# Attention layer of a two-block network: GpSimd's arithmetic moved to TensorE and VectorE, the gate and second modulation as products with a repeated column

## The chip, the cores and the metric

The program runs on one core of one Trainium2 chip. The metric is the device time of one execution in microseconds (us), lower is better. The engines go by the profile's names: PE is TensorE, PEld its weight loads, DVE VectorE, ACT ScalarE, POOL GpSimd, SP SyncE, which only issues transfers.

## The reference

The network has two blocks; the change lies in the first one, in the part ahead of its experts. With `D = 1024`, 512 tokens, and float32 throughout:

```python
mod = silu(c) @ w_ada + b_ada
shift1, scale1, gate1, shift2, scale2, gate2 = split(mod, 6)
h = rms_norm(x, norm1_g) * (1 + scale1) + shift1
proj = h @ w_in                              # six parts of 512 columns
o_a = dilated_mixture_attention(...)         # 8 heads of 64
o_b = differential_attention(...)            # 4 heads of 2 x 64
x = x + gate1 * (concat(o_a, o_b) @ w_out)
h2 = rms_norm(x, norm2_g) * (1 + scale2) + shift2
x = x + gate2 * moe_ffn(h2)                  # 32 experts, 4 for each token
```

`c` is one vector, so the last four parts of `mod` (gate1, shift2, scale2, gate2) are four vectors of 1024, each the product of a vector of 1024 with a 1024 x 1024 piece of `w_ada`. The kernel needs each of them repeated on all 128 partitions.

## The kernel before

The program has four phases; the change touches only `phase1`, the attention layer and the routing that follows it. What comes after (the experts, the second block's branches and its product-key layer) is the same code.

Float32 precision is kept in the large products by splitting each operand into a rounded part and a rest: ScalarE writes the rounded half (`wh`, `hTh`), another engine subtracts it from the original (`wl`, `hTl`), and TensorE makes three products (`mm3`, L167). Smaller products use plain float32.

**First part of phase 1 (about the first 72 us, written out in order).** The normalised input is transposed; for each of eight blocks of 128 columns `mod_block` (L383) computes the shift and scale. The shift goes through a VectorE product and sum, the scale through eight TensorE products with a two-column `sc2`, or for the five blocks in `PMOD` through GpSimd products and sums whose column sum TensorE takes in `mod_apply` (L418). Meanwhile the first 512 columns of `w_in` are multiplied.

**Second part (a planner).** `race` (L99) runs some thirty generators. Each yields a time on a modelled clock, in which every instruction is given a fixed cost per engine and per column; the generator with the lowest time goes next, and the order in which they emit instructions becomes the order of each engine's queue. Its lanes are: `ws.lane` (loads, rounds and splits `w_in`), `chunks` (ten half chunks of `w_in`, 96 products each), `norms`, the attention pairs (`pair_b` for the differential half, `pair_a` for the dilated one: `prep`, `scores`, `weigh`), `projects` and `third` (the product with `w_out`, times the gate, added to `x`), `roots`, `second` (the second normalisation with shift and scale) and routing.

**PSUM.** It has eight banks, which a counter deals out: `take(ps=...)` waits until enough are free. A half chunk takes two, a pair's scores two, its weighting three (a differential pair keeps two of them until its output has been turned), an output product one or two.

**The vectors of the second modulation.** `mods2` (L778) loads for each part eight weight tiles of 128 x 1024 (SP's queue, L786); GpSimd multiplies each with its column of `silu(c)` (L790; ScalarE at the even tiles of part 3, L788) and adds it to a running sum (L793). `mod_rows` (L799) then sums each part over the partitions by a product with ones (L809), and VectorE adds the bias row (L814). `projects` waits until three of the four parts are ready (L868); part 3 (gate2) begins when `x` is loaded again (L781).

**GpSimd's other work in this phase.** `WStream` (L196) takes an engine for each split: 22 of the 24 tiles of `w_in` (L341) and 5 of the 8 tiles of `w_out` (L836) are subtracted on GpSimd. So are most of the residual sums (L858, L915) and half of the sums of the second normalisation (L941).

The pages (30 tiles of 128 x 1024) are handed round by name: a load waits on SP's queue until the tile that it overwrites has been read.

Of the kernel before, what the change touches and what calls it, by code (L numbers as in the profile page):

```python
# [18 lines left out]
P = 128  # L19
# [286 lines left out]
def phase1(K):  # L306
# [31 lines left out]
    srcs = [wsrc(kp * 2, 2, first * 512, 512) for kp in range(4)]  # L338
    for c, half in HALVES:
        srcs += [wsrc(kq * 4, 4, c * 512 + half * 256, 256) for kq in range(2)]  # L340
    ws = WStream(K, srcs, 3, 2, eng=lambda i: nc.gpsimd if i < 4 or i >= 4 + len(EXTRA) and i % LOP == 0 else None)  # L341


    wada = []
# [38 lines left out]
    def mod_block(k):  # L383

        bm = K.bank("bm")
        w = wada[k][0]
        v.tensor_tensor(out=w, in0=w, in1=sc[:, :, None].to_broadcast([P, KC, P]), op=ALU.mult)
        acc = K.small([P, P], tag="mac", bufs=5)
        v.tensor_reduce(out=acc, in_=w.rearrange("p a c -> p c a"), axis=AX.X, op=ALU.add)
        w = wada[k][1]  # L390
        wada[k] = acc1 = None
        if k in PMOD:
            tt = nc.gpsimd.tensor_tensor
            tt(out=w, in0=w, in1=sc[:, :, None].to_broadcast([P, KC, P]), op=ALU.mult)
            tt(out=w[:, 0:4, :], in0=w[:, 0:4, :], in1=w[:, 4:8, :], op=ALU.add)
            tt(out=w[:, 0:2, :], in0=w[:, 0:2, :], in1=w[:, 2:4, :], op=ALU.add)
            acc1 = K.small([P, P], tag="mac", bufs=5)
            tt(out=acc1, in0=w[:, 0, :], in1=w[:, 1, :], op=ALU.add)
        else:
            for i in range(KC):  # L400
                nc.tensor.matmul(bm[:, 2:4], w[:, i, :], sc2[:, i, :], start=i == 0, stop=i == KC - 1)
        return (acc, acc1), bm

    m = [mod_block(0)]
    xT = [K.page(shape=[P, 2, T], name="xT") for _ in range(4)]
# [10 lines left out]
        return hT[k // 2][0][:, k % 2, :], hT[k // 2][1][:, k % 2, :]  # L416

    def mod_apply(k, acc, bm):  # L418
        for i, a in enumerate(acc):
            if a is not None:  # L420
                nc.tensor.matmul(bm[:, 2 * i:2 * i + 2], a, K.onesF[:, 0:2], start=True, stop=True)
        m = K.small([P, 2], tag="mcol", bufs=4)
        v.tensor_tensor(out=m, in0=bm[:, 0:4].rearrange("p (j t) -> p j t", t=2)[:, :, 0],
                        in1=bcol.rearrange("p (a k) -> p a k", a=2)[:, :, k], op=ALU.add)
        a1 = K.small([P, 1], tag="a1", bufs=4)
        v.scalar_tensor_tensor(a1, m[:, 1:2], 1.0, g1c[:, k:k + 1], op0=ALU.add, op1=ALU.mult)
        src = xT[k // 2][:, k % 2, :]
        hi, lo = hTk(k)
        act.activation(src, src, AF.Identity, bias=m[:, 0:1], scale=a1)
        act.copy(hi, src)  # L430
# [63 lines left out]
    def take(**n):  # L494

        while any(free[i] < n[i] for i in n):
            yield
        give(**{i: -n[i] for i in n})

    def give(**n):  # L500
        for i in n:
            free[i] += n[i]
# [274 lines left out]

    def mods2():  # L778

        for part in range(4):  # L780
            while part == 3 and len(xs) < NB:  # L781
                yield
            g = K.hold(name="gate2") if part == 3 else K.page(name="gm")
            for k in range(KC):
                w = K.page(name="wada")
                nc.sync.dma_start(out=w, in_=I["w_ada"][k * P:(k + 1) * P, (part + 2) * D:(part + 3) * D])  # L786
                if (part, k % 2) in MACT:
                    act.activation(w if k else g, w, AF.Copy, scale=sc[:, k:k + 1])  # L788
                else:
                    nc.gpsimd.tensor_tensor(out=w if k else g, in0=w, in1=sc[:, k:k + 1].to_broadcast([P, D]), op=ALU.mult)  # L790
                yield
                if k:
                    nc.gpsimd.tensor_tensor(out=g, in0=g, in1=w, op=ALU.add)  # L793
                yield
            gm.append(g)
            g = w = None
        yield

    def mod_rows(parts):  # L799
        while len(gm) < parts[-1] + 1:  # L800
            yield
        for part in parts:
            br = K.page(name="brow")
            act.dma_start(out=br, in_=row_bcast(I["b_ada_row"][:, part * D:(part + 1) * D], D))
            bs = []
            yield from take(ps=2)
            for half in range(2):
                bs.append(K.bank("gm"))
                nc.tensor.matmul(bs[half], K.onesF, gm[part][:, half * 512:half * 512 + 512], start=True, stop=True)  # L809
            yield  # L810
            yield
            for half in range(2):
                s = slice(half * 512, (half + 1) * 512)
                v.tensor_tensor(out=gm[part][:, s], in0=bs[half], in1=br[:, s], op=ALU.add)  # L814
            bs = br = None
            give(ps=2)
            yield
            if part == 2:
                g2r = K.page(name="g2r")
                act.dma_start(out=g2r, in_=row_bcast(I["norm2_g"], D))  # L820
                v.scalar_tensor_tensor(gm[2], gm[2], 1.0, g2r, op0=ALU.add, op1=ALU.mult)
                g2r = None
            rows.append(part)
            yield

    def lane(*gs):
        for g in gs:
            yield from g
# [4 lines left out]
            return [(dst.rearrange("p (k n) -> p k n", n=512), I["w_out"][k0 * P:(k0 + 2) * P, half * 512:half * 512 + 512].rearrange("(k p) n -> p k n", p=P))]  # L833
        return f

    wos = WStream(K, [osrc(k0 + j, half) for k0, js in ((4, (0, 2)), (0, (0,)), (2, (0,))) for half in range(2) for j in js], 2, 0, eng=lambda i: nc.gpsimd if i % WOE else None)  # L836
    xs = []

    def project(tb, half, wo, k0):
        hs = slice(half * 512, (half + 1) * 512)  # L840
        s = slice(tb * P, (tb + 1) * P)
        yield from take(ps=1)
        b = K.bank("wo")
        n = 2 * len(wo)
        for j in range(n):
            k = k0 + j
            ws = slice(j % 2 * 512, j % 2 * 512 + 512)
            K.mm3(b, (oT[k // 2][0][:, k % 2, s], oT[k // 2][1][:, k % 2, s]), (wo[j // 2][0][:, ws], wo[j // 2][1][:, ws]), j == 0, j == n - 1)
            if j == n - 1:
                yield  # L850
            elif j % 2:
                yield K.clock.free["tensor"] - PEA
        t = K.small([P, 512], tag="sq", bufs=2)
        v.tensor_tensor(out=t, in0=b, in1=gm[0][:, hs], op=ALU.mult)
        b = None
        give(ps=1)
        yield
        (v if k0 == 2 and half in ADDV else nc.gpsimd).tensor_tensor(out=xs[tb][:, hs], in0=xs[tb][:, hs], in1=t, op=ALU.add)  # L858
        t = None

    def projects():
# [26 lines left out]
    def third(tb):  # L888
# [18 lines left out]
        for half in range(2):  # L907
            yield ends[half]
            hs = slice(half * 512, (half + 1) * 512)
            t = K.small([P, 512], tag="sq", bufs=2)  # L910
            v.tensor_tensor(out=t, in0=bs[half], in1=gm[0][:, hs], op=ALU.mult)
            bs[half] = None
            give(ps=1)
            yield
            (v if half in ADDV else nc.gpsimd).tensor_tensor(out=xs[tb][:, hs], in0=xs[tb][:, hs], in1=t, op=ALU.add)  # L915
            yield
            act.activation(t, xs[tb][:, hs], AF.Square, accum_out=sums[i][0][:, tb % 2, half:half + 1])
            t = None
# [13 lines left out]
    def second(tb):  # L932
# [4 lines left out]
        for half in range(2):  # L937
            hs = slice(half * 512, (half + 1) * 512)
            v.scalar_tensor_tensor(h2[:, hs], xs[tb][:, hs], rss[tb // 2][:, tb % 2:tb % 2 + 1], gm[2][:, hs], op0=ALU.mult, op1=ALU.mult)
            yield  # L940
            (nc.gpsimd if half in H2P else v).tensor_tensor(out=h2[:, hs], in0=h2[:, hs], in1=gm[1][:, hs], op=ALU.add)  # L941
            yield None if half else K.clock.free["vector"]
        nc.sync.dma_start(out=K.h2d[tb * P:(tb + 1) * P, :], in_=h2)
        yield from take(ps=2)
# [54 lines left out]
    br = K.const([P, NE], name="br")  # L999
    nc.scalar.dma_start(out=br, in_=row_bcast(I["b_router"], NE))  # L1000
    B, A = [pair_b(h) for h in range(4)], [pair_a(p) for p in range(4)]
    race(K.clock, third(0), third(1), third(2), third(3), prefetch(), roots(0), roots(1), *[second(tb) for tb in range(NB)], ws.lane(WSA), split_out(), norms(), *(lane(B[0],A[0]),lane(B[1],A[1]),lane(B[2],A[2]),lane(B[3],A[3])), lane(chunks(), projects()), lane(mod_rows((0, 1, 2)), mod_rows((3,))), mods2())

    K.gate2 = gm[3]


CAP = 128
MACT = [(p, k) for p in range(3, 4) for k in range(1)]
ADDV, WOE = (1,), 3
HTV = ()  # L1010
RACT = True
PF, MLA = (8, 4, 4), (10, 6, 6, 1, 4)
# [4 lines left out]
UPACE, BV = 5.1, 3  # L1017
VB, VB2 = 4.0, 1.0
START = "a0 r01 n0 t0 a1 l0 r12 n1 t1 a2 l1 r23 n2 t2 a3 l2 w0 r34 n3 t3 l3"
LOP, ANRM, BNRM = 1, (0, 1), True  # L1020
HALVES = [(c, half) for c in (4, 5) for half in range(2)] + [(c, half) for half in range(2) for c in (0, 1, 2)]
SD, ES, QK, PEA, LAT = 1, 6, 2, 0.5, 0.2
H2P = (0,)
SMALL = 0.07
EXTRA = (5, 7)
WLA, WSA, WOA = 2, 1, 2
PMOD, ML, MA = (1, 2, 4, 5, 7), 3, 2
OFF = 10000.0
BIG = 4096.0

# [1614 lines left out]
```

## Time and profile before

| what | value |
|---|---|
| median of 3 runs | 3761.43 us (3748.43 to 3765.33) |
| the profiled execution | 3763.79 us, span 3762.0 us |
| PE busy | 3390.4 us (90%) |
| DVE busy | 3237.6 us (86%) |
| ACT busy | 1845.3 us (49%) |
| POOL busy | 1096.1 us (29%) |
| mean granted clock of TensorE | 0.947 |

A span is the time from the first to the last instruction. Busy time is the union of an engine's instructions; matmuls overlap, so a busy PE need not be at its peak. The clock is a share of 2.4 GHz. A row of instructions by group reads: line, engine, operation, what is written from what, shape, count | busy us, mean ns of one | idle time of the engine just before them and what ended it. A plain float32 product stands as two records in PE's rows.

### The profile page before, as it was taken

The numbers are of one execution on the slowest core, as the hardware profiler recorded it, in microseconds if no ns is written. First come the engines' busy times: TensorE is split into PE (matmuls) and PEld (weight loads), VectorE is DVE, ScalarE is ACT, GpSimd is POOL, SyncE is SP. The second block draws the span as 40 slices with busy tenths as digits, with TensorE's granted clock in tenths as the row PEclk, the third lists the DMA queues.
The fourth block names the chain that finished last, engine by engine and source line by source line (L and its number), as shares of the span: only waits on it lengthen the run. The fifth ranks groups of instructions, "written<-read, shape, count | busy, mean of one in ns | idle before, by whom it ended". The sixth has DMA issues, their size and how long they took to land. (4 is left out here: it accounts for less than half of the span.)

```text
span 3762.0 us, 51865 instructions
## 1 busy us (share of the span) xinstructions
PE 3390.4 (90%) x17053; PEld 2884.7 (77%) x17053; DVE 3237.6 (86%) x5729; ACT 1845.3 (49%) x2684; POOL 1096.1 (29%) x742
## 2 busy tenths in 40 slices
PE   6788789898999999999488899899889889999999
PEld 6776667667777888887377777798889889888887
DVE  7888789999898999998688776499999986799988
ACT  3233367666665677776234453333344445333333
POOL 5545501101110111111334440023223230456554
PEclk8878889999999999999699899899999999999999
DMA  6224369888997899997511112366779787999997
GB/s 216 85 85 157 129 232 327 295 306 304 334 317 252 319 356 368 351 366 282 182 51 51 51 52 100 104 208 216 237 241 309 251 291 248 334 340 342 345 340 260
DMA packets 453989, 906.05 MB, mean 241 GB/s; under 512 B 37810, under 2 KB 188978, under 8 KB 453586
## 3 DMA queue, kind: packets, MB, share of 16 engines
q1 hardware_dynamic: 333488, 692.66, 53.0%
q0 software_dynamic: 46368, 151.03, 11.1%
q10 hardware_dynamic: 73858, 59.00, 4.7%
q8 instruction: 136, 2.23, 0.2%
q14 instruction: 139, 1.14, 0.1%
HBM read 845.42 MB, written 74.96 MB: 245 GB/s over the span
## 5 line engine op out<-in xcount | busy, mean ns | idle before, releaser
L84 DVE TENSOR_TENSOR wl<-wr,wh 128x1024 fp32r<-128x1024 f32 x1106 | 1346.4, 1252 | 150.9 <-ACT wh L84 145.1
L84 ACT CAST wh<-wr 128x1024 fp32r<-128x1024 f32 x1133 | 1132.8, 1049 | 166.7 <-DVE wl L84 44.0
L84 PE MATMUL ft<-HT,wh 128*128 128x384 f32 (+1 forms) x2304 | 620.7, 350 | 4.9 <-ACT wh L84 4.9
L84 PE MATMUL out<-wh,HT 128*128 128x512 f32 x1536 | 473.3, 389 | 1.5 <-ACT HT L84 1.5
L84 PE MATMUL gu<-wl,exh 128*128 128x512 f32 x1056 | 417.6, 395 | 22.5 <-DVE wl L84 22.3
L84 PEld LDWEIGHTS ft<-HT,wh 128*128 128x128 f32 x2304 | 424.4, 193 | 14.8 <-ACT wh L84 5.5
L84 PE MATMUL ft<-HT,wl 128*128 128x384 f32 (+1 forms) x1152 | 402.8, 350 | 26.0 <-DVE wl L84 25.8
L84 PE MATMUL gu<-wh,exh 128*128 128x512 f32 x1056 | 420.6, 398 | 0.3 <-ACT wh L84 0.3
L84 PE MATMUL gu<-wh,exl 128*128 128x512 f32 x1056 | 413.7, 392 | 0.0
L84 PEld LDWEIGHTS out<-wh,HT 128*128 128x128 f32 x1536 | 288.2, 188 | 61.9 <-ACT HT L84 1.8
L2454 POOL DMA_INDIRECT ug<-in_peer_u,et x128 | 167.6, 1309 | 453.5 <-DVE sv L84 241.5
L84 PE MATMUL out<-wl,HT 128*128 128x512 f32 x768 | 298.8, 389 | 0.0
L2454 POOL DMA_INDIRECT ug<-in_peer_v,et x128 | 156.3, 1221 | 362.0 <-DVE x L84 240.0
L84 PEld LDWEIGHTS gu<-wl,exh 128*128 128x128 f32 x1056 | 199.5, 189 | 74.8 <-DVE wl L84 35.6
L84 PEld LDWEIGHTS ft<-HT,wl 128*128 128x128 f32 x1152 | 221.8, 193 | 40.7 <-DVE wl L84 35.6
L1317 POOL DMA_INDIRECT ybuf<-y,dst x33 | 93.3, 2827 | 505.1 <-DVE y L84 505.1
L84 PE MATMUL qkv<-wl,hTh 128*128 128x256 f32 (+1 forms) x736 | 227.2, 309 | 14.4 <-DVE wl L84 11.8
L1244 POOL DMA_INDIRECT xg<-h2d,tok x33 | 42.9, 1300 | 675.8 <-PE dn L84 478.1
L84 PE MATMUL qkv<-wh,hTh 128*128 128x256 f32 (+1 forms) x736 | 235.1, 319 | 2.0 <-ACT wh L84 2.0
L84 PEld LDWEIGHTS gu<-wh,exh 128*128 128x128 f32 x1056 | 199.8, 189 | 45.7 <-ACT wh L84 3.0
L84 PE MATMUL dn<-wl,ath 128*128 128x512 f32 x528 | 213.5, 404 | 22.9 <-DVE wl L84 20.2
L84 PEld LDWEIGHTS gu<-wh,exl 128*128 128x128 f32 x1056 | 199.3, 189 | 41.8
(481 smaller groups left out, 6952.8 us busy)
## 6 DMA issues: line engine op xcount, KB each, us to landing
wr<-in_w_gate_up SPq DMA_DIRECT2D x512, 512.0 KB, 6.5
wr<-in_w_down SPq DMA_DIRECT2D x256, 512.0 KB, 6.4
wr<-in_u_t SPq DMA_DIRECT2D x128, 512.0 KB, 4.3
wr<-in_peer_v SPq DMA_DIRECT2D x128, 512.0 KB, 6.1
wr<-in_w_in SPq DMA_DIRECT2D x68, 512.0 KB, 3.5
wada<-in_w_ada SPq DMA_DIRECT2D x48, 512.0 KB, 4.3
Sd<-us ACTq DMA_DIRECT2D x128, 192.0 KB, 4.7
Gd<-gst ACTq DMA_DIRECT2D x12, 2048.0 KB, 15.7
```

The lines of the kernel that those rows point to most:

```text
L84: return f(*a, **kw)
L1244: nc.gpsimd.indirect_dma_start(out=self.xg, out_offset=None, in_=K.h2d[:, :], in_offset=bass.IndirectOffsetOnAxis(ap=self.tok[:, :1], axis=0),
L1317: st = nc.gpsimd.indirect_dma_start(out=self.rows, out_offset=bass.IndirectOffsetOnAxis(ap=self.dst[:, :1], axis=0), in_=y, in_offset=None ...
L2454: nc.gpsimd.indirect_dma_start(out=r, out_offset=None, in_=tab, in_offset=bass.IndirectOffsetOnAxis(ap=et[:, m:m + 1], axis=0), bounds_che ...
```

## The change

GpSimd no longer does any arithmetic in phase 1. The five mod blocks of `PMOD` use the TensorE products of the others. All splits, residual sums and modulation sums go to VectorE. `mods2` is rewritten: a tile `scb` holds `silu(c)` with each column repeated 128 times, and for each part eight weight tiles are multiplied by it on TensorE in plain float32, 512 columns at a time, accumulating in two PSUM banks that are taken before the first and given back after the last; the result stands on all partitions at once. Two tiles are loaded ahead (`MLD`), and a tile's products are at least 6 us of the planner's clock after the previous ones (`MPACE`). The bias row and the gain row are loaded at the start of a part. `mod_rows` is gone.

```diff
-    ws = WStream(K, srcs, 3, 2, eng=lambda i: nc.gpsimd if i < 4 or i >= 4 + len(EXTRA) and i % LOP == 0 else None)
+    ws = WStream(K, srcs, 3, 2)
...
-        wada[k] = acc1 = None
-        if k in PMOD:
-            tt = nc.gpsimd.tensor_tensor
-            tt(out=w, in0=w, in1=sc[:, :, None].to_broadcast([P, KC, P]), op=ALU.mult)
-            tt(out=w[:, 0:4, :], in0=w[:, 0:4, :], in1=w[:, 4:8, :], op=ALU.add)
-            tt(out=w[:, 0:2, :], in0=w[:, 0:2, :], in1=w[:, 2:4, :], op=ALU.add)
-            acc1 = K.small([P, P], tag="mac", bufs=5)
-            tt(out=acc1, in0=w[:, 0, :], in1=w[:, 1, :], op=ALU.add)
-        else:
-            for i in range(KC):
-                nc.tensor.matmul(bm[:, 2:4], w[:, i, :], sc2[:, i, :], start=i == 0, stop=i == KC - 1)
-        return (acc, acc1), bm
+        wada[k] = None
+        for i in range(KC):
+            nc.tensor.matmul(bm[:, 2:4], w[:, i, :], sc2[:, i, :], start=i == 0, stop=i == KC - 1)
+        return acc, bm
...
     def mods2():
...
+        scb = K.page(shape=[P, KC, P], name="scb")
+        v.tensor_copy(scb, sc[:, :, None].to_broadcast([P, KC, P]))
+        t = 0.0
+        pages = []
+
+        def fetch(i):
+            part, k = divmod(i, KC)
+            w = K.page(name="wada")
+            nc.sync.dma_start(out=w, in_=I["w_ada"][k * P:(k + 1) * P, (part + 2) * D:(part + 3) * D])
+            pages.append(w)
+
         for part in range(4):
             while part == 3 and len(xs) < NB:
                 yield
...
             br = K.page(name="brow")
             act.dma_start(out=br, in_=row_bcast(I["b_ada_row"][:, part * D:(part + 1) * D], D))
...
+            for i in range(MLD):
+                fetch(part * KC + i)
+            t = max(t + MPACE, K.clock.end + MPACE)
+            yield t
+            yield from take(ps=2)
+            bs = [K.bank("gm") for _ in range(2)]
+            for k in range(KC):
+                if k + MLD < KC:
+                    fetch(part * KC + k + MLD)
+                w = pages.pop(0)
+                for half in range(2):
+                    nc.tensor.matmul(bs[half], scb[:, k, :], w[:, half * 512:half * 512 + 512], start=k == 0, stop=k == KC - 1)
+                w = None
+                t = max(t + MPACE, K.clock.end)
+                yield t if k < KC - 1 else None
+            g = K.hold(name="gate2") if part == 3 else K.page(name="gm")
+            for half in range(2):
+                s = slice(half * 512, (half + 1) * 512)
+                v.tensor_tensor(out=g[:, s], in0=bs[half], in1=br[:, s], op=ALU.add)
...
-    wos = WStream(K, [...], 2, 0, eng=lambda i: nc.gpsimd if i % WOE else None)
+    wos = WStream(K, [...], 2, 0)
...
-        (v if k0 == 2 and half in ADDV else nc.gpsimd).tensor_tensor(out=xs[tb][:, hs], in0=xs[tb][:, hs], in1=t, op=ALU.add)
+        v.tensor_tensor(out=xs[tb][:, hs], in0=xs[tb][:, hs], in1=t, op=ALU.add)
...
-            (v if half in ADDV else nc.gpsimd).tensor_tensor(out=xs[tb][:, hs], in0=xs[tb][:, hs], in1=t, op=ALU.add)
+            v.tensor_tensor(out=xs[tb][:, hs], in0=xs[tb][:, hs], in1=t, op=ALU.add)
...
-            (nc.gpsimd if half in H2P else v).tensor_tensor(out=h2[:, hs], in0=h2[:, hs], in1=gm[1][:, hs], op=ALU.add)
+            v.tensor_tensor(out=h2[:, hs], in0=h2[:, hs], in1=gm[1][:, hs], op=ALU.add)
...
-    race(K.clock, ..., lane(mod_rows((0, 1, 2)), mod_rows((3,))), mods2())
+    race(K.clock, ..., mods2())
...
+MLD, MPACE = 2, 6.0
```

## Rows read from the trace of the kernel before

**Rows 1.** By stretch, us: length, busy PE, PEld, DVE, ACT, POOL; clock; DMA; GB/s

```profile
0.00:72.00 72.00, 41.80 (x180) 35.82 (x180) 52.85 (x71) 25.44 (x35) 43.86 (x32) 0.86 0.63 233
72.00:108.00 36.00, 35.96 (x267) 34.65 (x268) 29.03 (x40) 12.24 (x20) 19.78 (x10) 0.95 0.42 130
72.00:345.00 273.00, 222.94 (x1439) 201.47 (x1440) 227.81 (x441) 88.69 (x205) 137.98 (x63) 0.82 0.31 102
345.00:470.00 125.00, 98.33 (x468) 77.94 (x466) 93.96 (x221) 46.09 (x118) 74.76 (x52) 0.83 0.42 149
```

**Rows 2.** Instructions by group, VectorE, 0 to 470 us

```profile
L84 DVE TENSOR_SCALAR e<-e,rd 128x128 f32<-128x128 f32 (+3 forms) x48 | 44.2, 978 | 0.1
L84 DVE TENSOR_TENSOR raw<-raw,qrs 128x256 f32<-128x256 f32 x32 | 31.7, 1040 | 0.1
...
L84 DVE TENSOR_TENSOR wada<-wada,silc 128x1024 f32<-128x1024 f32 x8 | 16.3, 2041 | 0.0
...
L84 DVE TENSOR_TENSOR rqa<-qrs 128x16 f32<-128x16 f32 x24 | 12.5, 520 | 0.5
...
L84 DVE TENSOR_TENSOR rsqa<-obr 128x4 f32<-128x4 f32 x12 | 10.1, 838 | 0.2
L84 DVE SCALAR_TENSOR_TENSOR rsqa<-rsqa,rsqv 128x4 f32<-128x4 f32 x15 | 9.6, 639 | 0.3
...
L84 DVE TENSOR_TENSOR h<-h,gm 128x512 f32<-128x512 f32 x4 | 2.7, 680 | 0.0
```

**Rows 3.** Timeline of VectorE: start us, us, instruction; places up to 312 us

```profile
32.56 1.21 DVE L84 TENSOR_TENSOR wada<-wada,silc 128x1024 f32<-128x1024 f32 x1
...
102.16 0.17 DVE L84 TENSOR_TENSOR rqa<-qrs 128x16 f32<-128x16 f32 x1
...
106.25 7.40 DVE L84 TENSOR_TENSOR raw<-raw,qrs 128x256 f32<-128x256 f32 x4
...
117.88 1.43 DVE L84 TENSOR_TENSOR raw<-raw,qrs 128x256 f32<-128x256 f32 x4
...
303.16 7.08 DVE L84 TENSOR_SCALAR e<-e,rd 128x128 f32<-128x128 f32 x4
...
310.85 1.26 DVE L84 TENSOR_SCALAR e<-e,rd 128x128 f32<-128x128 f32 x4
```

**Rows 4.** Timeline of GpSimd, 110 to 122 us

```profile
110.52 2.52 POOL L84 TENSOR_TENSOR gm<-gm,wada 128x1024 f32<-128x1024 f32 x1
119.18 2.37 POOL L84 TENSOR_TENSOR wl<-wr,wh 128x1024 fp32r<-128x1024 f32 x1 [6.15 <-ACT wh L84]
```

**Rows 5.** Waits of TensorE, 0 to 470 us: total us, times, longest

```profile
PE ot L84 <- DVE op L84: 15.2, 2, 14.6
...
PE h2t L84 <- POOL h L84: 9.1, 1, 9.1
```

**Rows 6.** Instructions by group, GpSimd, 0 to 470 us

```profile
L84 POOL TENSOR_TENSOR wl<-wr,wh 128x1024 fp32r<-128x1024 f32 x27 | 67.3, 2494 | 107.5 <-ACT wh L84 79.3 <-DVE rsqa L84 19.8 <-issue 8.4
```

**Rows 7.** The page, costliest groups: the same subtraction on VectorE, whole span

```profile
L84 DVE TENSOR_TENSOR wl<-wr,wh 128x1024 fp32r<-128x1024 f32 x1106 | 1346.4, 1252 | 150.9 <-ACT wh L84 145.1
```

**Rows 8.** Timeline of TensorE, 345 to 359 us

```profile
345.19 1.88 PE L84 MATMUL gm<-gm,onesF 128*128 128x512 f32 x4
...
354.86 3.78 PE L84 MATMUL gm<-gm,onesF 128*128 128x512 f32 x4
```

**Rows 9.** Instructions by group, TensorE, 0 to 470 us

```profile
L84 PE MATMUL bm<-silc,wada 128*128 128x2 f32 x48 | 8.9, 317 | 16.7 <-DMA wada<-in_w_ada 16.7
```

**Rows 10.** The page, DMA issues: count, KB each, median us to landing

```profile
wada<-in_w_ada SPq DMA_DIRECT2D x48, 512.0 KB, 4.3
```

**Rows 11.** The page, 40 slices of the span: TensorE's busy tenths

```profile
PE   6788789898999999999488899899889889999999
```

**Rows 12.** Instructions by group, TensorE, 180 to 200 us

```profile
L84 PE MATMUL ob<-vh,pt 128*128 128x128 f32 x20 | 3.8, 279 | 0.0
L84 PE MATMUL s<-qkh,qkh 64*128 64x256 f32 (+3 forms) x7 | 3.1, 444 | 0.0
```

More of the change, by code (lines that the diff above doesn't have):

```diff
@@ L418, in mod_apply @@
     def mod_apply(k, acc, bm):
-        for i, a in enumerate(acc):
-            if a is not None:
-                nc.tensor.matmul(bm[:, 2 * i:2 * i + 2], a, K.onesF[:, 0:2], start=True, stop=True)
+        nc.tensor.matmul(bm[:, 0:2], acc, K.onesF[:, 0:2], start=True, stop=True)
         m = K.small([P, 2], tag="mcol", bufs=4)
@@ L782, in mods2 @@
                 yield
[L783 to L802, printed above, removed]
             br = K.page(name="brow")
             act.dma_start(out=br, in_=row_bcast(I["b_ada_row"][:, part * D:(part + 1) * D], D))
[L805 to L817, printed above, removed]
             if part == 2:
@@ L820, in mod_rows @@
                 act.dma_start(out=g2r, in_=row_bcast(I["norm2_g"], D))
-                v.scalar_tensor_tensor(gm[2], gm[2], 1.0, g2r, op0=ALU.add, op1=ALU.mult)
+            for i in range(MLD):
[17 more added lines that the diff above has]
+                v.tensor_tensor(out=g[:, s], in0=bs[half], in1=br[:, s], op=ALU.add)
+            bs = br = None
+            give(ps=2)
+            if part == 2:
+                v.scalar_tensor_tensor(g, g, 1.0, g2r, op0=ALU.add, op1=ALU.mult)
                 g2r = None
+            gm.append(g)
             rows.append(part)
+            g = None
             yield
@@ L834, in osrc @@
         return f
-    wos = WStream(K, [osrc(k0 + j, half) for k0, js in ((4, (0, 2)), (0, (0,)), (2, (0,))) for half in range(2) for j in js], 2, 0, eng=lambda i: nc.gpsimd if i % WOE else None)
+    wos = WStream(K, [osrc(k0 + j, half) for k0, js in ((4, (0, 2)), (0, (0,)), (2, (0,))) for half in range(2) for j in js], 2, 0)
     xs = []
@@ L1001, in phase1 @@
     B, A = [pair_b(h) for h in range(4)], [pair_a(p) for p in range(4)]
-    race(K.clock, third(0), third(1), third(2), third(3), prefetch(), roots(0), roots(1), *[second(tb) for tb in range(NB)], ws.lane(WSA), split_out(), norms(), *(lane(B[0],A[0]),lane(B[1],A[1]),lane(B[2],A[2]),lane(B[3],A[3])), lane(chunks(), projects()), lane(mod_rows((0, 1, 2)), mod_rows((3,))), mods2())
+    race(K.clock, third(0), third(1), third(2), third(3), prefetch(), roots(0), roots(1), *[second(tb) for tb in range(NB)], ws.lane(WSA), split_out(), norms(), *(lane(B[0],A[0]),lane(B[1],A[1]),lane(B[2],A[2]),lane(B[3],A[3])), lane(chunks(), projects()), mods2())
     K.gate2 = gm[3]
 CAP = 128
-MACT = [(p, k) for p in range(3, 4) for k in range(1)]
-ADDV, WOE = (1,), 3
+MLD, MPACE = 2, 6.0
 HTV = ()
@@ L1019 @@
 START = "a0 r01 n0 t0 a1 l0 r12 n1 t1 a2 l1 r23 n2 t2 a3 l2 w0 r34 n3 t3 l3"
-LOP, ANRM, BNRM = 1, (0, 1), True
+ANRM, BNRM = (0, 1), True
 HALVES = [(c, half) for c in (4, 5) for half in range(2)] + [(c, half) for half in range(2) for c in (0, 1, 2)]
 SD, ES, QK, PEA, LAT = 1, 6, 2, 0.5, 0.2
-H2P = (0,)
 SMALL = 0.07
@@ L1026 @@
 WLA, WSA, WOA = 2, 1, 2
-PMOD, ML, MA = (1, 2, 4, 5, 7), 3, 2
+ML, MA = 3, 2
 OFF = 10000.0
```

## The prediction

> **What bounds the kernel now.** I read the page first: TensorE and VectorE are both busy for most of the span, GpSimd for little of it. The diff touches only the first attention layer, which ends when the router starts, some 470 us into the span. So the second view is busy time by stretch, cut at 72 us (the end of the first product), 345 us (the last head of the differential half has been turned) and 470 us [rows 1]. In the long stretch from 72 to 345 us VectorE is busy 228 of 273 us and TensorE 223, at a mean clock of 0.82. GpSimd is busy 138 us, and the layer has no other heavy user of it. In no stretch is any engine full except TensorE from 72 to 108 us: 35.96 of 36 us, clock 0.95. That is what TensorE does when nothing holds it up.
>
> The third view, VectorE by groups [rows 2], shows what is odd. Instructions on 4 or 16 columns last 0.5 to 0.8 us on average, and 256 columns last 1.04 us. The timeline tells why [rows 3, 4]. Four products `raw<-raw,qrs` from 106.25 us on take 7.40 us while GpSimd runs its two-input instructions; the same four from 117.88 us on, with GpSimd idle for 6.15 us until 119.18, take 1.43 us. Four `e<-e,rd` take 7.08 us at 303 us, and 1.26 us at 311 us. So much of VectorE's busy time is waiting for GpSimd. TensorE waits behind it in turn: 15.2 us of its idle time is for `op`, computed by just such a VectorE chain, and 9.1 us for a sum on GpSimd itself [rows 5].
>
> **What the waiting is worth.** Count times (mean minus undisturbed duration), with the undisturbed one from rows 3:
> - `e<-e,rd`: 48 x (0.978 - 0.32) = 31.6 us (1.26 us for four widths gives 0.32)
> - `raw`: 32 x (1.040 - 0.36) = 21.8
> - `rqa<-qrs`: 24 x (0.520 - 0.17) = 8.4
> - the two `rsqa` groups: 12 x (0.838 - 0.17) + 15 x (0.639 - 0.17) = 8.0 + 7.0
> - `wada<-wada,silc`: 8 x (2.041 - 1.21) = 6.6
>
> Together 83 us of VectorE time up to 470 us. Smaller groups of the same kind are left out, so this is a lower bound.
>
> **What is added to VectorE.** 27 subtractions `wl` leave GpSimd [rows 6], at 1.25 us each on VectorE [rows 7]: 33.8 us. 20 residual sums and 4 sums of the second modulation at 0.68 us, the `h<-h,gm` row [rows 2]: 16.3 us. One broadcast copy of 1024 columns is not in the trace: between 0.6 us (half of 1.21) and 1.25 us (two inputs of that width); I take 1.2, the nearer form. Together 51 us, so VectorE gets at least 32 us lighter.
>
> **What is added to TensorE.** Each of four vectors of 1024 is now summed by 8 x 2 float32 products of 512 columns: 64 products. The same form stands in the trace as `gm<-gm,onesF`, two records to a product: four records take 1.88 us at the full clock, thus 0.94 us a product, and 3.78 us at the half clock, 1.89 us a product [rows 8]. Parts 0 to 2 put 48 x 0.94 = 45 us into the middle stretch. Part 3 puts 16 x 0.94 = 15 us after 345 us, from where the 8 column-sum products (7.5 us) go away. The five mod blocks of the first stretch take 8 products, two records each, 80 in all; 48 such records were busy 8.9 us [rows 9], so 15 us.
>
> The Trainium skill (Perfetto Trace Analysis, Engine Utilization) says that float32 in two passes halves TensorE's output rate. By it a product of 512 columns would take an estimated 2 x 512 / 2.4 GHz = 0.43 us and the 48 would cost 20 us. The trace disagrees: 0.94 us stands in a row of the same form, so this reading gets no chance of its own.
>
> **What moves on the queues.** The 32 loads `wada` stay on SP's queue, two ahead now, at least 6 us of the planner's time apart; one lands in 4.3 us [rows 10], so a TensorE product waiting for one should find it there. If it doesn't, everything behind it on TensorE waits too, where earlier only GpSimd waited; 0 to 4.3 us per late load, and I take 0 because of the lead. The bias row's loads on ACT's queue are issued before the products rather than after, which can only help. One to two more 4 KB pages of 30 are held (the broadcast, a second weight tile); if a page were missing, SP's queue would hold the loads of `w_in` behind it. I take 0 for the same lead. Of GpSimd's 257 us up to 470 us [rows 1] none is left on a path but its wait for `h`, counted below.
>
> **The sum by stretches.** 0 to 72 us: VectorE loses 6.6 us and gets 4 x 1.25 = 5.0; TensorE has 30 us idle for the 15 us. I take -2.
>
> 72 to 345 us: VectorE falls from 228 to about 180, so TensorE becomes the tighter one. Its 223 us at clock 0.82 are 223 x 0.82 / 0.95 = 192 us at the clock of the undisturbed stretch; with 45 us added, 237 us. It had 50 us idle. With none left the stretch takes 237 us (-36), with half 262 (-11), with all 287 (+14). I take 15 us of idle time, because the waits that I see in it end at VectorE chains stretched several times over, and because the new products don't depend on those chains: 252 us, -21.
>
> 345 to 470 us: the wait of 9.1 us for GpSimd's `h` mostly goes; VectorE gets 5 + 20 + 4 instructions (23 us) against about a fifth of its 83 us; TensorE's net 7.5 us have 27 us of idle time around them. I take -5.
>
> Together -28 us. The expert stage that follows has TensorE at 8 to 9 tenths throughout [rows 11], so an earlier start is passed on, and I take it in full. The profiled execution took 3763.8 us with a span of 3762.0; 3763.8 - 28 = 3735.8. The median of the runs is 2.4 us below the profiled one: 3733 us.
>
> **The rivals.**
> *TensorE gives it all back.* Its idle time is a matter of dependencies, not of slow VectorE work: 25 to 45 us of it stay, and the middle stretch ends between -11 and +9. For it: 45 us of products are added to an engine already busy four fifths of the time. Against it: the idle waits end at VectorE and GpSimd. Time: 3745 to 3765.
>
> *TensorE packs fully.* No idle time is left in the middle stretch, and the last one loses 8: -46, 3715 us. For it: 72 to 108 us ran so. Against: many short chains meet later.
>
> *PSUM banks run short, slower.* The new products hold two of eight banks for eight weight tiles, some 48 us for each part by the 6 us pace, where the old ones held two for one short product. From 180 to 200 us scores `s` and weighting `ob` run side by side [rows 12]; by the code these hold 2 and 3 banks, and a half chunk in work 2 more. With two more there are nine, so a score or a weighting must wait for the other while a part lasts. Each overlap lost costs up to the 20 us of that stretch. Two lost cancel the gain (3745); three, one for each part, give 3733 + 60 = 3793. For it: the count of banks. Against: chunk products and the new ones fill TensorE meanwhile, and the bound on the path is only felt if the head chain sets the end.
>
> The Trainium skill (Perfetto Trace Analysis, Optimization Strategy) names repeated bubbles on the engine that should be full as a sign of too little PSUM or SBUF. No run here shows it yet; it is what I would look for.
>
> *The waiting isn't GpSimd's.* If VectorE's long instructions came from something else, 51 us would be added to it, a part on the path: +30 us, 3791. The paired rows speak against it.
>
> **Chances.** 0.5% is 19 us, about what a measurement of this kernel can tell from no change. Forecast 0.50, full packing 0.12, TensorE gives it back 0.23, banks 0.12, not GpSimd 0.03. Faster by over 0.5% (under 3742): 0.62; same: 0.23; slower (over 3780): 0.15. Range 3692 to 3785: below it VectorE would need more than the bound of 83 us off the path, above it three overlaps lost.
>
> **What would show it.** Right: no GpSimd arithmetic before 470 us; `rqa` and `rsqa` at 0.17 us and `raw` near 0.4 in the means; the last turned head at about 320 us rather than 345; TensorE's idle time in the middle under 25 us and its clock above 0.85. Wrong: TensorE idle as much as before beside undisturbed VectorE instructions (banks or dependencies), or `s` and `ob` no longer in the same stretch (banks), or TensorE waiting for `wada`.

## The result, and the profile after

The changed kernel takes 3704.1 us (median of 4 runs, 3700.4 to 3711.7) where the kernel before took 3763.4 us beside it (4 runs, 3748.4 to 3774.5): a ratio of 0.9849, 95% interval 0.9829 to 0.9869, 59 us faster. Timed again (run `e12_after_again` below) it was 0.9849 again. The forecast was 3733 us, with 3715 as one of its rivals.

The profiled execution took 3711.7 us, with a span of 3709.6 us. The 40 slices of its page:

```profile
PE   7999699898999999995688999999888889999999
...
PEclk9999799999999999997799999999999999999999
```

The second to fourth slice (93 to 371 us) are now at 9 tenths, where the kernel before has 7, 8 and 8 [rows 11].

The last turned differential head, at which the forecast cut the layer, comes in another order now (its `ot` at 226 us, 118 us earlier, where the layer ends 62 us earlier), so here all traces are cut at three events: TensorE resumes after its wait for the last `hTl` of the first product; the first product `wo` of the output projection; the first expert product `gu`, which ends the layer. Stretches of the kernel before, then of the changed kernel (columns as in rows 1: length, busy PE, PEld, DVE, ACT, POOL, clock, DMA share, GB/s):

```profile
0.00:72.04 72.04, 41.80 (x181) 35.83 (x181) 52.85 (x71) 25.48 (x35) 43.86 (x32) 0.86 0.63 233
72.04:359.87 287.83, 234.72 (x1484) 208.70 (x1484) 239.21 (x462) 97.88 (x218) 150.13 (x68) 0.82 0.34 112
359.87:485.30 125.43, 90.02 (x438) 74.17 (x437) 92.16 (x226) 42.48 (x112) 63.78 (x48) 0.80 0.34 120
```

```profile
0.00:66.54 66.54, 47.35 (x250) 42.23 (x250) 45.58 (x75) 25.47 (x35) 0.85 (x7) 0.90 0.67 248
66.54:298.30 231.76, 228.57 (x1554) 191.19 (x1554) 158.53 (x474) 94.63 (x214) 0.00 (x0) 1.00 0.42 133
298.30:423.30 125.00, 98.66 (x481) 76.46 (x480) 99.26 (x262) 43.87 (x113) 7.29 (x13) 0.84 0.38 133
```

The layer ends 62.0 us earlier: 5.5 us come from the first stretch, 56.1 from the middle, 0.4 from the last. The two profiled executions as a whole are 52.1 us apart (3763.8 and 3711.7), because the stretch behind the last `gu` took 8.2 us longer in the second (2005.6 against 1997.4); two profiles of the changed kernel alone differ there by as much (see the last experiments). In the middle TensorE is busy 228.6 of 231.8 us at the full clock, GpSimd not at all, and VectorE has fallen from 239 to 159 us. The expert stage behind it is as long as before (1280.7 us from the first to the last `gu`, 1279.3 before), so the gain is passed on.

VectorE by groups, 0 to 423 us, of the changed kernel (as rows 2):

```profile
L84 DVE TENSOR_TENSOR wl<-wr,wh 128x1024 fp32r<-128x1024 f32 x35 | 42.6, 1221 | 7.7 <-ACT wh L84 7.7
L84 DVE TENSOR_TENSOR x<-x,sq 128x512 f32<-128x512 f32 x24 | 16.5, 689 | 0.6
L84 DVE TENSOR_SCALAR e<-e,rd 128x128 f32<-128x128 f32 (+3 forms) x48 | 15.3, 382 | 0.1
L84 DVE TENSOR_TENSOR raw<-raw,qrs 128x256 f32<-128x256 f32 x32 | 11.8, 420 | 0.2
...
L84 DVE TENSOR_TENSOR rqa<-qrs 128x16 f32<-128x16 f32 x24 | 4.1, 173 | 0.6
...
L84 DVE TENSOR_TENSOR rsqa<-obr 128x4 f32<-128x4 f32 x12 | 1.9, 160 | 0.2
L84 DVE COPY scb<-silc 128x1024 f32<-128x1024 f32 x1 | 0.7, 684 | 0.0
```

`e` fell from 978 to 382 ns, `raw` from 1040 to 420, `rqa` from 520 to 173, `rsqa` from 838 to 160 [rows 2]: near the undisturbed durations that the forecast had taken (0.32, 0.36, 0.17 and 0.17 us).

TensorE's waits in the changed kernel, 0 to 423 us:

```profile
PE bm L84 <- DMA wada<-in_w_ada: 16.4, 1, 16.4
PE L L84 <- DVE ohs L84: 10.4, 1, 10.4
PE h2t L84 <- DVE h L84: 9.0, 2, 7.5
```

The 15.2 us for `op` [rows 5] are gone. The 9.1 us for `h` on GpSimd are hardly less: 9.0 us in two waits, the longest 7.5, and they end on VectorE now.

### The profile page after: what moved, and what is told of

The parts are those of the page before. It is cut to its first block, busy times and chain, and to the rows that moved or that the text cites. A ratio compares the mean times of both kernels' runs of the same rounds, so it can differ in the third digit from the quotient of the medians.

```text
span 3709.6 us, 52069 instructions
## 1 busy us (share of the span) xinstructions
PE 3397.7 (92%) x17235; PEld 2876.2 (78%) x17235; DVE 3149.6 (85%) x5781; ACT 1843.3 (50%) x2680; POOL 848.1 (23%) x615
## 5 line engine op out<-in xcount | busy, mean ns | idle before, releaser
L84 DVE TENSOR_TENSOR wl<-wr,wh 128x1024 fp32r<-128x1024 f32 x1133 | 1371.6, 1246 | 165.1 <-ACT wh L84 158.4
L84 PE MATMUL qkv<-wl,hTh 128*128 128x256 f32 (+1 forms) x736 | 218.5, 297 | 13.6 <-DVE wl L84 13.6
L84 PE MATMUL qkv<-wh,hTl 128*128 128x256 f32 (+1 forms) x736 | 217.6, 296 | 0.8 <-DVE hTl L84 0.8
L84 PE MATMUL dn<-wh,ath 128*128 128x512 f32 x528 | 214.8, 407 | 0.0
```

Source lines behind the costliest of these rows:

```text
L84: return f(*a, **kw)
```

## The experiments

GpSimd's two-input arithmetic could have cost time in two ways. **Stretching** (the forecast): while GpSimd reads, VectorE's instructions wait, and TensorE behind them. **Queue** (the rival): GpSimd's own results came late, or the new products fill TensorE's gaps better, and the stretching is hidden. The first eight runs undo or isolate one piece each; "later" is the first `gu` against the changed kernel's 423.3 us.

### Private GpSimd work that nobody waits for

```diff
+        dm = K.page(name="dm")
+        nc.nc.gpsimd.memset(dm, 1.0)
...
+                for _ in range(2):
+                    nc.nc.gpsimd.tensor_tensor(out=dm, in0=dm, in1=dm, op=ALU.mult)
```

The second run has four `memset(dm, 1.0)` in the loop in place of the two products: GpSimd is nearly as long at work, but only writes.

> The changed kernel with 64 more GpSimd products of 1024 columns on a page of their own (two before each weight tile of the vectors), which nobody reads and which the planner isn't told of, so that every other queue keeps its order. 'Stretching': some 120 to 150 us of GpSimd time, rqa's mean above 0.3 us, TensorE idle for 15 us or more between 61 and 296 us, first expert product at 435 to 470 us. 'Queue': nobody waits for them, so everything stays within 3 us of the changed kernel (423 us).

> The same with 128 fills of 1024 columns on GpSimd (four before each weight tile), some 120 us of GpSimd time that writes SBUF and reads none. If any GpSimd use stretches VectorE, rqa's mean rises as with the two-input products and the first expert product starts at 435 to 470 us. If it is GpSimd's reading that VectorE's two-input instructions wait for, rqa and raw stay at their undisturbed 0.17 and 0.4 us, and the first expert product stays at 423 to 430 us; e<-e,rd, with one input and a column of scalars, may still be longer.

Measured: 3765.2 and 3710.5 us (kernel before: 3756.0 on the same chip). The first `gu` came at 487.3 us with two-input products (64 us later, and 2 us later than in the kernel before), at 431.0 us with fills (7.7 later). Both came later than expected (435 to 470 and 423 to 430 us). GpSimd's rows, one of each run:

```profile
L805 POOL TENSOR_TENSOR dm<-dm 128x1024 f32<-128x1024 f32 x64 | 134.0, 2093 | 5.0
```

```profile
L805 POOL MEMSET dm<- 128x1024 f32 x128 | 123.5, 965 | 7.4
```

VectorE by groups, 0 to 470 us, with two-input products, then with fills:

```profile
L84 DVE TENSOR_TENSOR raw<-raw,qrs 128x256 f32<-128x256 f32 x32 | 34.2, 1116 | 0.2
...
L84 DVE TENSOR_SCALAR e<-e,rd 128x128 f32<-128x128 f32 (+3 forms) x48 | 15.3, 382 | 0.1
L84 DVE TENSOR_TENSOR rqa<-qrs 128x16 f32<-128x16 f32 x24 | 14.2, 593 | 0.6
...
L84 DVE TENSOR_SCALAR qrs<-rqa 128x16 int32<-128x16 int32 x8 | 6.1, 761 | 0.2
```

```profile
L84 DVE TENSOR_SCALAR e<-e,rd 128x128 f32<-128x128 f32 (+3 forms) x48 | 21.3, 542 | 0.1
...
L84 DVE TENSOR_TENSOR raw<-raw,qrs 128x256 f32<-128x256 f32 x32 | 11.8, 419 | 0.2
...
L84 DVE TENSOR_SCALAR qrs<-rqa 128x16 int32<-128x16 int32 x8 | 5.4, 672 | 0.2
...
L84 DVE TENSOR_TENSOR rqa<-qrs 128x16 f32<-128x16 f32 x24 | 4.1, 172 | 0.6
```

With the two-input work (56 to 196 us) the 14 `raw` that began beside it took 2.01 us on average, about one whole GpSimd instruction (2.09), the 18 others 0.42. The 48 `e`, with one input, all came after it and show nothing; of the one-input `qrs<-rqa`, three began beside it and took 1.75 us against 0.17. With the fills (57 to 189 us) the 16 `raw` beside them took 0.42 us like the rest, while 12 one-input `e` took 1.02 us against 0.38, and five `qrs<-rqa` 0.98 against 0.17, one fill (0.97) or so. So GpSimd instructions that read stretch VectorE's two-input instructions, and fills don't; GpSimd instructions with a single input weren't run. The products alone, without any result of GpSimd's being late, cost as much as the whole change gained. The waits that it makes on TensorE (middle stretch, two-input run):

```profile
PE qt L84 <- DVE raw L84: 30.9, 4, 23.4
PE qkv L84 <- DVE wl L84: 7.2, 1, 7.2
PE s L84 <- DVE qkl L84: 6.6, 2, 5.5
```

The Trainium skill (SBUF — State Buffer, Who interferes with whom) says that a VectorE instruction with two SBUF inputs contends with GpSimd instructions that read and not with those that only write, that one-input scalar and copy forms can contend with GpSimd too, and that the loser waits for the whole instruction. Both runs agree, with the durations just named.

### Each piece put back alone

The four vectors back on GpSimd, as in the kernel before, with the rest of the change kept:

```diff
-                for half in range(2):
-                    nc.tensor.matmul(bs[half], scb[:, k, :], w[:, half * 512:half * 512 + 512], start=k == 0, stop=k == KC - 1)
...
+                    nc.gpsimd.tensor_tensor(out=w if k else g, in0=w, in1=sc[:, k:k + 1].to_broadcast([P, D]), op=ALU.mult)
...
+                if k:
+                    nc.gpsimd.tensor_tensor(out=g, in0=g, in1=w, op=ALU.add)
```

> The changed kernel with the four vectors summed on GpSimd as before (32 products, 28 sums, then the product with ones); splits and residual sums stay on VectorE. Theory 'stretching' (VectorE instructions last longer while GpSimd does two-input arithmetic, and the gain is their return to normal length): the mean of rqa goes from 0.17 us back to 0.3 to 0.5, TensorE's idle time between 61 and 296 us comes back in part, and although 48 products leave TensorE the first expert product starts later than in the changed kernel (423 us), at 435 to 455. Theory 'queue' (the gain came from instructions no longer waiting in GpSimd's queue for slow results): VectorE's means stay at 0.17, 41 us of products are gone from a full TensorE, and the first expert product starts earlier, at 385 to 410.

Measured: 3755.3 us (before 3756.0), the first `gu` at 475.6 us, 52 later (435 to 455 was expected of stretching), although TensorE had 64 products less and only 8 column-sum products more. Its middle stretch:

```profile
71.37:357.21 285.84, 235.72 (x1476) 205.80 (x1477) 223.63 (x490) 100.43 (x230) 108.35 (x48) 0.84 0.35 113
```

The vectors are most of the effect, and with the private work this settles the two theories: stretching explains both runs, while the queue theory has nothing for 64 us from work without a result. The splits and the five mod blocks, each put back alone:

```diff
-    ws = WStream(K, srcs, 3, 2)
+    ws = WStream(K, srcs, 3, 2, eng=lambda i: nc.gpsimd if i < 4 or i >= 4 + len(EXTRA) else None)
...
-    wos = WStream(K, [...], 2, 0)
+    wos = WStream(K, [...], 2, 0, eng=lambda i: nc.gpsimd if i % 3 else None)
```

> The changed kernel with 27 subtractions wl on GpSimd again (22 of w_in, 5 of w_out), nothing else. 'Stretching': 67 us of GpSimd instructions come back, about a quarter of what there was; rqa's mean rises to 0.2 to 0.35 us, and the first expert product starts at 428 to 445 us although VectorE has 34 us less of its own. 'Queue': TensorE's products wait for wl behind GpSimd; means stay at 0.17, first expert product at 420 to 435.

```diff
+        if k in PMOD:
+            tt = nc.gpsimd.tensor_tensor
+            tt(out=w, in0=w, in1=sc[:, :, None].to_broadcast([P, KC, P]), op=ALU.mult)
...
+        else:
+            for i in range(KC):
+                nc.tensor.matmul(bm[:, 2:4], w[:, i, :], sc2[:, i, :], start=i == 0, stop=i == KC - 1)
```

> The changed kernel with the five mod blocks of the first stretch on GpSimd again (27 us of GpSimd time before 70 us). 'Stretching': VectorE's wada products go from 1.2 to about 2 us, the end of the first product moves from about 61 to 66 to 72 us and the first expert product from 423 to 428 to 434. If the first stretch is set by the arrival of data or by TensorE, both stay within 3 us or come earlier, since 80 records (15 us) leave TensorE.

Measured: 3706.6 and 3709.6 us; the first `gu` at 432.8 (9.5 later) and 428.9 (5.6 later). In the total neither can be told from the changed kernel; the layer's end shows both (two profiles of one and the same kernel have it 0.5 and, with gate2 on VectorE, 2.3 us apart). The mod blocks stretch `wada` from 1.22 to 1.65 us. The splits leave the theories unparted: `rqa` rose from 0.17 to 0.26 us and `e` from 0.38 to 0.60, `raw` stayed at 0.42, and TensorE waited 2.6 us for a `wl` on GpSimd itself; 432.8 lies in both expected ranges. The parts, 52 + 9.5 + 5.6 = 67 us, come near the 62 of the whole; the residual sums weren't put back alone.

### TensorE in the middle: more work, less work, shorter holds

Every new product twice (so the four vectors are doubled, the routing changes, and only what lies ahead of the first `gu` can be compared):

```diff
-                    nc.tensor.matmul(bs[half], scb[:, k, :], w[:, half * 512:half * 512 + 512], start=k == 0, stop=k == KC - 1)
+                    for r in range(2):
+                        nc.tensor.matmul(bs[half], scb[:, k, :], w[:, half * 512:half * 512 + 512], start=k == 0 and r == 0, stop=k == KC - 1 and r == 1)
```

> The changed kernel with each of the 64 float32 products of the vectors made twice into the same sum (the vectors come out doubled). Between 61 and 296 us TensorE is busy 233 of 235 us in the changed kernel. If TensorE's amount of work sets that stretch, 48 more products at 0.86 to 0.94 us lengthen it by 41 to 45 us, part 3 adds up to 15, and the first expert product starts at 460 to 480 us instead of 423. If the products lie in time that TensorE would have idled away, it starts at 423 to 435.

Measured: the first `gu` at 479.6 us, 56 later; 3819.8 us in all. The middle stretch:

```profile
65.54:339.72 274.18, 273.20 (x1661) 210.22 (x1662) 164.06 (x487) 93.54 (x212) 0.00 (x0) 1.00 0.35 114
```

With no gap and the full clock, the added products make 273.2 - 228.6 = 44.6 us of busy time, and the stretch is 42.4 us longer. It has 200 product records where the changed kernel has 96, so 52 products more (four of part 3 came ahead of the first `wo`), about 0.86 us each. TensorE's work is now the length of this stretch.

All four vectors on VectorE instead, one instruction per weight tile (and, in a second run, parts 0 to 2 so, gate2 on TensorE, with one load ahead):

```diff
-                for half in range(2):
-                    nc.tensor.matmul(bs[half], scb[:, k, :], w[:, half * 512:half * 512 + 512], start=k == 0, stop=k == KC - 1)
+                if k:
+                    v.scalar_tensor_tensor(g, w, sc[:, k:k + 1], g, op0=ALU.mult, op1=ALU.add)
+                else:
+                    act.activation(g, w, AF.Copy, scale=sc[:, k:k + 1])
```

> The changed kernel with the four vectors summed on VectorE by one instruction per weight tile (scaled by a column and added, 28 in all, ScalarE scales the first of each part), then a product with ones; GpSimd stays idle. 28 x 1.22 = 34 us go to VectorE (160 of 235 us busy in the middle stretch), 36 us leave TensorE there and 9 us later. If TensorE's amount of work sets the middle stretch: first expert product at 390 to 410 us, total 3670 to 3690 us. If what counted was only to free VectorE, it is at 423 or later, total 3700 or more. If GpSimd's stretching is the whole story, both give the same within 5 us.

> Parts 0 to 2 summed on VectorE as in the run before, part 3 by TensorE products as in the changed kernel, one weight tile loaded ahead instead of two. If TensorE's work sets the time in the middle, it gains as much there as with all four on VectorE (first expert product at 390 to 415 us); after it VectorE, which got the residual sums, is spared 8.5 us for 14 us on TensorE: within 8 us of the run before either way.

Measured: 3701.8 us (0.9838, 0.9811 to 0.9865) and 3699.8 us (0.9832, 0.9811 to 0.9854): both within the changed kernel's interval. The first `gu` came at 420.0 and 419.4 us: not at 390 to 415, as it should if TensorE's work set the time, but within the 5 us of "GpSimd's stretching is the whole story". The middle and last stretch with all four on VectorE:

```profile
66.60:308.12 241.52, 224.28 (x1514) 198.87 (x1514) 184.96 (x525) 102.57 (x234) 0.00 (x0) 0.91 0.40 130
308.12:420.03 111.91, 80.26 (x409) 67.01 (x407) 99.62 (x238) 37.64 (x95) 7.29 (x13) 0.83 0.42 144
```

TensorE has less to do in the middle, yet the middle is 10 us longer; the last stretch is 13 us shorter. Part of that is order: 45 score records (`s`) that the changed kernel has behind its first `wo` lie ahead of it here, and with parts 0 to 2 alone on VectorE the middle takes 210.9 us and the last stretch 142.4. The tables, worked out from the traces, therefore give the middle and then both stretches together: idle is length less busy; the clock's loss is half of the busy time that lies where the granted clock is 1.2 GHz; what is left is TensorE's work at 2.4 GHz.

| middle stretch, us | length | idle | lost to the clock | work |
|---|---|---|---|---|
| before | 287.8 | 53.1 | 37.6 | 197.1 |
| changed | 231.8 | 3.2 | 0 | 228.6 |
| vectors back on GpSimd | 285.8 | 50.1 | 33.8 | 201.9 |
| private two-input work | 289.5 | 48.8 | 11.1 | 229.7 |
| private fills | 238.8 | 5.0 | 5.1 | 228.7 |
| products twice | 274.2 | 1.0 | 0 | 273.2 |
| vectors on VectorE | 241.5 | 17.2 | 20.8 | 203.5 |
| parts 0 to 2 on VectorE | 210.9 | 9.8 | 11.6 | 189.5 |

| middle and last stretch, us | length | idle | lost to the clock | work |
|---|---|---|---|---|
| before | 413.2 | 88.5 | 49.9 | 274.8 |
| changed | 356.7 | 29.5 | 8.0 | 319.2 |
| vectors on VectorE | 353.4 | 48.9 | 28.8 | 275.8 |
| parts 0 to 2 on VectorE | 353.4 | 40.5 | 25.2 | 287.7 |

In the middle the change adds 31.5 us of work and takes away 49.9 us of idle time and 37.6 us of clock loss: 56.0 us. Over both stretches the kernel with the vectors on VectorE has the work of the kernel before and is 59.8 us shorter (39.6 us of idle time, 21.1 of clock loss): what counts is that GpSimd no longer does them; which of the other two engines does makes 3 to 4 us. Against that kernel the changed one has 43.5 us more of work and is only 3.3 us longer, with 19.4 us less idle time and 20.8 us less clock loss.

The hold of the two PSUM banks halved:

```diff
-MLD, MPACE = 2, 6.0
+MLD, MPACE = 2, 3.0
```

> The changed kernel with the pace of the new products halved (at least 3 us of the planner's clock between two weight tiles instead of 6), so that each part holds its two PSUM banks for about half as long. The work is the same. Banks (the rival of the prediction, kept open because scores and weightings visibly take turns with the chunk while a part lasts): a held bank delays the head chain, so halving the hold brings the first product of the output projection forward by 5 to 15 us, from 298 to 283 to 293 us. TensorE full (my theory): it is 99 percent busy at the full clock from 61 to 296 us, so another order of the same work ends at the same time: first output product at 295 to 302 us, first expert product at 420 to 427 us, total 3698 to 3712 us. A third outcome: weight tiles are now wanted twice as fast and products wait for their loads (over 5 us of TensorE waits for wada beyond the 16 us of the first stretch): then later than 302 us.

Measured: 3705.6 us, the first `wo` at 300.3 and the first `gu` at 426.5 us, TensorE busy 231.5 of 232.9 us in the middle. A part's products now lie within 23 to 29 us (45 to 49 in the changed kernel, parts 0 to 2), and nothing came forward: the hold of the banks cost nothing that halving it gives back.

### Gate2 alone off TensorE

```diff
-MLD, MPACE = 2, 6.0
+MLD, MPACE, DVP = 2, 6.0, (3,)
...
+                if part in DVP:
+                    if k:
+                        v.scalar_tensor_tensor(g, w, sc[:, k:k + 1], g, op0=ALU.mult, op1=ALU.add)
+                    else:
+                        act.activation(g, w, AF.Copy, scale=sc[:, k:k + 1])
```

> The changed kernel with part 3 alone (gate2) taken off TensorE: one VectorE instruction per weight tile (product and running sum together, 7 of them, the first a scaled copy on ScalarE) and two column-sum products. TensorE loses 16 products less 2, 12 us of work, in the stretch from the first output product to the first expert product (125 us long both in the kernel before and in the changed one, where I had forecast a gain of 5). Gate2 on the path (TensorE sets this stretch too): the stretch becomes 8 to 12 us shorter, 113 to 117 us. VectorE sets it (my theory: from 357 to 382 us the changed kernel's VectorE has no gap, its products and residual sums back to back, and the second normalisation waits for their end): not shorter, 122 to 132 us, since VectorE gets 7 more instructions of about 1.2 us. The stretch before is untouched: first output product at 295 to 302 us. Total 3698 to 3715 us.

> The kernel of the run before this (gate2's part on VectorE, the other three parts on TensorE), timed in five rounds beside the changed kernel and the kernel before on one chip. Its single time was 3689.1 us, 79 us under the kernel before on the same chip, but only 4.4 us of what separates it from the changed kernel lay ahead of the first expert product (418.9 against 423.3 us); the rest lay in code that the two share. If the gain is that of the attention layer alone (my theory): median 3696 to 3702 us where the changed kernel has 3700 to 3706, a difference of 2 to 8 us that the intervals hardly part. If the later phases really run shorter after it (the layout of instructions or pages behind it): 3686 to 3693 us, and the changed kernel 3700 to 3706, a difference of 10 to 18 us.

> The changed kernel itself, timed in five rounds on the same chip as the run above, so that the two can be compared directly. Both theories: 3700 to 3706 us, a ratio to the kernel before of 0.983 to 0.987. Its profiled execution should show the first expert product at 420 to 427 us again; how far the stretch behind the last expert product (2005.6 us in the profile of the changed kernel, 1997.4 in that of the kernel before) differs between two executions of the same program tells how much of a difference there is spread: over 8 us means that it carries nothing.

Measured: 3689.1 us in a single run (before 3767.8); then, in five rounds on one chip, 3697.3 us (3696.1 to 3704.1; 0.9829, 0.9807 to 0.9851), with the changed kernel at 3706.0 (3700.8 to 3712.3; 0.9849, 0.9828 to 0.9871). The last stretch of the timed run:

```profile
297.89:416.58 118.69, 87.62 (x452) 71.55 (x452) 105.96 (x269) 44.20 (x114) 7.29 (x13) 0.82 0.39 139
```

Both runs have it near 118.8 us, 6.2 less than the changed kernel, which neither expectation for it had. From the first `wo` to the end of the last it takes 73.6 us (79.5 in the changed kernel), and the rest is the same. TensorE has 13 us less work there, and 6.2 of them shorten the stretch: gate2's products are about half on the path. VectorE, busy for 106 us instead of 99, doesn't set this stretch; I had thought that it did. The medians are 8.7 us apart, 2.6 us more than the layer's own gain in these two profiles (416.6 against 422.7 us), and the intervals overlap: a version probably better than both, by an amount that these runs don't settle. The single run's 3689 is no measure of it: behind the last `gu` two executions of the changed kernel differ by 8.1 us (2005.6 and 1997.5).

## Why the prediction was right, and where its size was off

The sign, the mechanism and the range were right; the 28 us were less than half of the 59, and what happened is the rival "TensorE packs fully" (-46), to which the forecast gave a chance of 0.12, and more.

- **What the waiting is worth.** VectorE's busy time in the layer fell from 384.2 to 303.4 us. The added work is 27 `wl` at 1.22, 24 sums at 0.69 and a copy of 0.68: 50.2 us, where the forecast had 51. So 131 us were taken away; its 83 were the lower bound that it said, since `qrs`, `obr` and other small groups were left out.
- **First stretch, -2.** Measured -5.5. The wait for the last `hTl` fell from 2.48 to 0.75 us. The vectors put back alone bring the end of this stretch to 71.4 us again, the mod blocks put back alone to 70.4, from 66.5; the forecast had looked at the mod blocks' share (`wada`) alone.
- **Middle, -21.** This is the step that failed. The forecast's 252 us (to 345 us) and the 15 us from there to the first `wo`, left as they were, make 267; measured were 231.8. Of these 36 us, 11.8 are the idle time: 15 taken, 3.2 measured. Another 9.6 are the clock: the old work, 223 x 0.82 = 183 us, was taken at 0.95, and with TensorE full it was granted 1.00 (192.4 - 182.8). A further 6.3 are idle time and clock loss in those 15 us, of which 8.6 were work. The last 8.0 are work: 228.6 us measured, where the forecast's terms and these 8.6 make 236.5. Two slips of the forecast cancel in it: the granted clock under the busy time gives 188.5 us of old work and not 183, since a stretch's mean clock counts its idle time too, and six column-sum products (5.6 us) that lay ahead of the first `wo` went away there. What remains is mostly 15 score records that lie behind the first `wo` now (4.3 us less of `s`) and the price of a product, 0.94 taken and 0.89 measured (2.6 us for the 48).
- **"Many short chains meet later".** This was the reason to leave 15 us idle, and it was wrong. The chains were short as soon as their instructions were, and in the trace `qkv` chunks, which depend on none of them, stand between their products.
- **Last stretch, -5.** Measured -0.4. "The wait of 9.1 us for GpSimd's `h` mostly goes": from the end of the last `wo` to `h2t` it took 9.1 us before and 7.5 now. In both timelines VectorE's last `rs` chain and its `h` stand between the last residual sum and `h2t`; in the runs without GpSimd there it took 6.6 to 8.7 us, so which engine adds the shift behind them matters little. "TensorE's net 7.5 us have 27 us of idle time around them": half of gate2's products were on the path. The 15 score records that moved behind the first `wo` add to this stretch, too.

What would show it, as listed: no GpSimd arithmetic in the layer, `rqa`, `rsqa` and `raw` as said, under 25 us idle and a clock above 0.85 in the middle (3.2 us, 1.00). The landmark was badly chosen: the last turned head moved by twice as much as the layer's end, to 226 us, so that it shows a new order more than the speed. The signs of being wrong didn't appear: TensorE waited for `wada` only at the start (16.4 us, 16.7 before), and `s` and `ob` still run side by side while a part is summed (24 and 30 records from 140 to 160 us).

**The rivals.** "TensorE gives it all back" fell with 3.2 us of idle time. "PSUM banks run short" fell with the halved hold; its price was also mis-added, since two overlaps of 20 us lost make 3773 and not 3745. "The waiting isn't GpSimd's" fell with the private work: nothing but GpSimd's products was added, and the 62 us were back, where fills brought 7.7. What stays open is why the vectors put back cost 34 us of clock loss and the private work only 11, at the same idle time. The traces differ in how the idle time lies: 11 waits with the private work, 23.4 us in the longest, and 19 with the vectors, 13.9 us in the longest, with TensorE granted 1.2 GHz for 55 and for 94 us. Many shorter waits may cost more of the clock than a few long ones; no run tries that apart.

## What to carry to other kernels

Price an off-path GpSimd instruction by what it does to VectorE's two-input instructions beside it, not by its own waits: compare one VectorE form in the timeline with GpSimd busy and idle. Where TensorE is busy four fifths at a low clock, work moved onto it can cost less than its duration: here 43.5 us of it cost 3.3 us, with less idle time and a granted clock of 0.95 instead of 0.88 over the two stretches. Once the stretch is full, further products cost their whole time (44.6 us of them, 42.4 us more). Cut both traces at the same events, and choose events that a planner can't reorder; the first `wo` isn't quite one, so add up both sides of it.

## What the runs showed that I had not expected

- Less work on TensorE hardly helped: 275.8 us of it took 353.4 us at a granted clock of 0.88, and 319.2 us took 356.7 at 0.95.
- Fills by GpSimd aren't free either: one-input `TENSOR_SCALAR` instructions on VectorE went from 0.38 to 1.02 us beside them (`e`) and from 0.17 to 0.98 (`qrs`), two-input ones (`raw`, `rqa`) didn't change.
- The broadcast copy of 1024 columns took 0.68 us, near the low end of its bounds (0.6 to 1.25), not the 1.2 taken.
